# Fewer sevenfold pairs in the first three blocks of the up-projection, and the convolution queued ahead of the split

## The chip, the cores and the metric

The kernel runs on one core of a Trainium2 chip. The metric is the device time of one execution in microseconds; less is better. Three runs of the kernel before took 1755.26, 1757.42 and 1757.81 us, a median of 1757.42 us.

## What is computed

One layer of a hybrid decoder block on 256 tokens of width 2048, all in float32: a norm, one combined input projection, a gated linear recurrence and a dilated attention, two merge gates and an output projection, and then the part that the change touches:

```python
def conv_ffn(u, w_up, conv_w, conv_b, w_down):
    hup = u @ w_up                                   # 2048 x 11264
    hc = causal_depthwise_conv(hup, conv_w) + conv_b # width 3, along the tokens
    a, b = hc[..., :D_FF], hc[..., D_FF:]            # D_FF = 5632
    return (jax.nn.gelu(a) * b) @ w_down             # 5632 x 2048
```

It is added to the residual, and a last norm follows.

## The kernel before, in words

All weights are read from HBM once, in 1 MB **units** of sixteen 128 x 128 blocks, in the order in which they are used (`stream_spec`). A buffer `raw` holds a unit; there are three. Before use each unit is **split**: ScalarE writes a rounded high part (`hi`), VectorE subtracts it from the weights and writes the low part (`lo`). TensorE forms each product as three matmuls of 512 columns, low by high, high by high, high by low (lines 543 to 545 for w_up, 490 to 492 for w_down), so only the third needs the low part of the weights.

The up-projection runs over 11 **blocks**. A block takes 512 columns of each of the two halves of w_up, and its contraction in 8 **pairs** of 128 rows each, a unit per pair. A pair of type P is 8 products (24 matmuls); its unit is split in two pieces `hl`. A pair of type S is the sevenfold form: 7 products (21 matmuls) of sums of the weight blocks. `split_s` (line 292) forms them with four additions of 128 x 512 on VectorE (lines 304 to 309, the first one named `q`) and splits four pieces `sa`, `se`, `sf` (128 x 1024 each) and `sg` (128 x 512). All 11 blocks alternate S and P by `UP_PAIRS = "SPSPSPSP"`; `up_order` sets the order of the pairs in the first two. The activations of every pair are prepared once, in the form of its type, by `operands` (line 512), while the output projection w_out runs. The products gather in seven PSUM banks, and `unfold` (line 549) reads the seven sums after a block into `c11` to `c22`, three of them by a DMA that accumulates (line 567, POOL's queue).

Some blocks are followed by units of w_down, type P, for hidden blocks that are ready: two after blocks 1 and 2, four after each later one, more at the end. Units are numbered through: block 0 of w_up is 168 to 175, block 1 176 to 183, block 6 232 to 239.

The hidden values of a block are finished while later units run, by a generator, `hidden_side` (line 988): it waits `HIDDEN_WAIT = 3` units, and then takes a step per unit: two steps `ua t0`, `ua t1` for the first half and two `ub t0`, `ub t1` for the second (`convolve`, line 970). In a step TensorE transposes four 128 x 128 blocks into PSUM bank 8 (line 978), ScalarE makes two scaled copies (line 981) and VectorE adds the two other taps to each (lines 982 and 983). There is one bank 8, so the next step's transposes must wait for VectorE. After the four steps come a GELU, a product (line 1001) and the split of the result `ff` (line 1005, through 282).

`begin_unit(u)` (line 370) comes ahead of each unit's matmuls: it writes the splits of the units up to `u + LOOKAHEAD` (2), starts the load of unit u + 3, and then lets the generator take its step:

```python
    def begin_unit(u):
        for v in range(u, u + LOOKAHEAD + 1):
            split(v)
        load(u + LOOKAHEAD + 1)
        pump(SIDE_US)
```

A scheduler of the framework sets the final order on each engine, by the program's order and its own estimates; `in_turn` pins instructions of an engine behind a given one of that engine. Split pieces go through a ring of six buffers (`pair_tile`, line 284), so a split can lead TensorE by about two units at most.

Of the kernel before, what the change touches and what calls it, by code (L numbers as in the profile page):

```python
# [15 lines left out]
ALU = mybir.AluOpType  # L16
# [32 lines left out]
START_X = {0: ((2, 4),), 1: ((4, 8),), 2: ((8, 12),), 3: ((12, 16),)}  # L49


def up_order(b):


    return {0: (1, 3, 0, 5, 2, 4, 7, 6), 1: (1, 0, 3, 2, 5, 4, 6, 7)}.get(b, tuple(range(KD // 2)))

# [1 line left out]
def stream_spec():  # L60
    spec, modes = [], {}

    def stat(name, col, k0, nk):
        for k in range(k0, k0 + nk):
            spec.append((name, k * P, col))

    def mov(name, col, k0, nk):
        for k in range(k0, k0 + nk):
            for c in range(4):
                spec.append((name, k * P, col + c * P))  # L70

    def pairs(name, n1, n2, k0, modes_of, order):

        for i in order:
            mode = modes_of[i]
            assert len(spec) % UNIT == 0
            k2, k1 = k0 + 2 * i, k0 + 2 * i + 1
            modes[len(spec) // UNIT] = mode
            blocks = [(k1, n1), (k2, n1), (k2, n2), (k1, n2)] if mode == "S" else [(k1, n1), (k2, n1), (k1, n2), (k2, n2)]
            for k, n in blocks:  # L80
                for c in range(4):
                    spec.append((name, k * P, n + c * P))

    o_q, o_f, o_i, o_g = 0, 2048, 4096, 6144
    o_aq, o_ak, o_av, o_ga, o_gb = 8192, 9728, 11264, 12800, 14848
    for k in range(KD):
        for base in (o_av, o_aq):
            for c in range(AH):
                spec.append(("w_in", k * P, base + c * P))
    for h in range(AH):  # L90
        stat("w_in", o_ak + h * P, 0, KD)
    for j in range(1, AG):
        for base in (o_aq, o_ak):
            for h in range(AH):
                stat("w_in", base + (j * AH + h) * P, 0, KD)
        mov("w_in", o_av + j * 512, 0, KD)
    for g in range(NGRP):
        for base in (o_f, o_q):
            for h in range(HG):
                stat("w_in", base + (g * HG + h) * P, 0, KD)  # L100
        mov("w_in", o_i + g * 512, 0, KD)
        mov("w_in", o_g + g * 512, 0, KD)
    for base in (o_ga, o_gb):
        for j in range(NJ):
            mov("w_in", base + j * 512, 0, KD)
    for j in range(NJ):
        mov("w_proj_b", j * 512, 0, AH)
        mov("w_proj_a", j * 512, 0, KD)
    for j in range(NJ):
        mov("w_out", j * 512, 0, KD)  # L110
    for b in range(NBLK):
        pairs("w_up", b * 512, DFF + b * 512, 0, UP_PAIRS, up_order(b))
        for j, b0, b1 in DOWN.get(b, ()):
            mov("w_down", j * 512, b0 * FB, (b1 - b0) * FB)

    for j in range(NJ):
        mov("w_down", j * 512, (NBLK - 1) * FB, FB)
    assert len(spec) % UNIT == 0
    return spec, modes
# [56 lines left out]
def hybrid_block(ctx, tc, x_p, x_t, weights, g1, gf, params, c_rope, c_mask0, c_mask1, c_level, out):  # L176
# [52 lines left out]

    raws, splits, late = {}, {}, {}  # L230
    ring = [0]
    last = [None, None]

    @contextmanager
# [133 lines left out]
        debt[0] = 0.0  # L368

    def begin_unit(u):  # L370
        for v in range(u, u + LOOKAHEAD + 1):
            split(v)
        load(u + LOOKAHEAD + 1)
        pump(SIDE_US)

    def next_pair():

# [134 lines left out]
    def operands(a, mode, i, name):  # L512

        f = a.rearrange("p k m t -> p (k m) t")
        if mode == "S":
            x = stage(f"{name}x32_{i}").rearrange("p (b t) -> p b t", b=4)
            vec.tensor_tensor(x[:, 0:2], f[:, 3:4].to_broadcast([P, 2, P]), f[:, 1:3], op=ALU.subtract)
            vec.tensor_tensor(x[:, 2], f[:, 2], x[:, 0], op=ALU.subtract)
            vec.tensor_tensor(x[:, 3], f[:, 0], x[:, 2], op=ALU.subtract)
            parts = w4([2, 3, P], f"{name}s{i}", F32R), w4([2, 4, P], f"{name}x{i}", F32R)  # L520
            two_parts(parts[0][:, 0], parts[0][:, 1], f[:, 0:3])
            two_parts(parts[1][:, 0], parts[1][:, 1], x)
            names = ("a12", "a22", "a11"), ("x1", "x3", "x2", "x4")
        else:
            d = stage(f"{name}d32_{i}")[:, :T].rearrange("p (k t) -> p k t", k=2)
            vec.tensor_tensor(d, a[:, :, 0], a[:, :, 1], op=ALU.subtract)
            parts = w4([2, 4, P], f"{name}a{i}", F32R), late["hv"].tile([P, 2, 2, P], F32R, tag=f"{name}d", name=f"{name}d{i}", bufs=sum(m != "S" for m in UP_PAIRS))
            two_parts(parts[0][:, 0], parts[0][:, 1], f)
            two_parts(parts[1][:, 0], parts[1][:, 1], d)
            names = ("a12", "a22", "a11", "a21"), ("d2", "d1")  # L530
        return {n: (t[:, 0, j], t[:, 1, j]) for t, ns in zip(parts, names) for j, n in enumerate(ns)}
# [438 lines left out]
    def convolve(ups, c0, t, name):  # L970


        for i in range(2):
            pt = late_bank(8, f"{name}t{i}").rearrange("p (c t) -> p c t", c=2)
            for c in range(2):
                for m in range(2):
                    n = (2 * i + c) * P
                    pe.transpose(pt[:, c, m * P : (m + 1) * P], ups[m][:, n : n + P], ident)
            for c in range(2):
                d, s, col = t[:, 2 * i + c], pt[:, c], c0 + 2 * i + c  # L980
                act.activation(d, s, AF.Identity, bias=pc("cb", col), scale=pc("cw2", col))
                vec.scalar_tensor_tensor(d[:, 1:], s[:, : T - 1], pc("cw1", col), d[:, 1:], op0=ALU.mult, op1=ALU.add)
                vec.scalar_tensor_tensor(d[:, 2:], s[:, : T - 2], pc("cw0", col), d[:, 2:], op0=ALU.mult, op1=ALU.add)
            yield SIDE_US

    ff = {}
# [1 line left out]
    def hidden_side(b, sums):  # L988

        c11, c21, c12, c22 = unfold(sums, rstd2, neg2, f"up{b}")  # L990
        for _ in range(HIDDEN_WAIT):
            yield SIDE_US
        a, g = (late["pool"].tile([P, FB, T], F32, tag="uc", name=f"u{n}{b}", bufs=2) for n in "ab")
        yield from convolve((c11, c21), b * FB, a, f"ua{b}")
# [14 lines left out]
        return t[:, 0, m * P : (m + 1) * P], t[:, 1, m * P : (m + 1) * P]  # L1009

    for b in range(NBLK):
        sums = sevenfold(hv, UP_PAIRS, up_order(b), f"up{b}")
        drain()
        side.append(hidden_side(b, sums))
        pump(0.0001)
        for j, b0, b1 in DOWN.get(b, ()):
            pst = moving(ff_parts, b0 * FB, (b1 - b0) * FB, f"dn{b}_{j}", [late_bank(i, f"dn{b}_{j}_{i}") for i in ((4, 3) if j % 2 else (1, 5))])
            for m in range(2):
                if b == NBLK - 1:
                    vec.tensor_tensor(ht[j][:, m], ht[j][:, m], pst[m], op=ALU.add)  # L1020
                else:
                    t = stage(f"dns{b}_{j}_{m}")
                    act.activation(t, pst[m], AF.Copy)
                    nc.gpsimd.dma_start(ht[j][:, m], t, accum_op=ALU.add)
# [84 lines left out]
```

## Time and profile before

| | |
|---|---|
| median of three runs | 1757.42 us |
| profiled execution, its own time | 1757.53 us |
| its span | 1755.8 us |
| TensorE busy | 1725.8 us, 98% of the span |
| VectorE busy | 1302.6 us, 74% |
| ScalarE busy | 992.8 us, 57% |
| DMA | 346.13 MB, mean 197 GB/s |
| mean granted clock of TensorE | 0.995 |

The profiled execution took 1757.53 us, 0.11 us more than the median of the runs; its span, from the first to the last instruction, is 1755.8 us, and 1.7 us lie outside it. TensorE's line gives little away, since it is busy nearly throughout: what is left are its waits, and the stretches in which the clock was below full speed. VectorE's 74% is a mean; in the up-projection, from 1008 us to the end, it is far busier than earlier.

### The profile page before, as it was taken

The page shows a single profiled execution, that of the slowest core. Times are in us where ns is not written, and L with a number is a line of the kernel's source. Part 1 is how long each engine was busy: PE and PEld are TensorE (multiplying, and loading weights), DVE is VectorE, ACT ScalarE, POOL GpSimd, SP SyncE. Part 2 cuts the span into 40 slices and gives each one's busy share as a digit, 9 for nine tenths or more (in the row PEclk, how much of TensorE's full clock was granted, in tenths as well). Part 3 has the DMA queues.
Part 4 walks back from the last instruction along what each step waited for, and adds up shares of the span by engine and source line. Part 5 has one row for each costly group of instructions (what it writes and reads, how often), then busy time and mean ns, then how long its engine had stood idle before and what let it go on. Part 6 is the DMA issues. An engine that isn't in the chain of part 4 may idle for free.

```text
span 1755.8 us, 21521 instructions
## 1 busy us (share of the span) xinstructions
PE 1725.8 (98%) x8340; PEld 1440.9 (82%) x8340; DVE 1302.6 (74%) x1628; ACT 992.8 (57%) x1259; POOL 70.2 (4%) x94
## 2 busy tenths in 40 slices
PE   9999999999999999999999999799999999999998
PEld 7888888888888888888888877688878878788886
DVE  7765575877768675445665699899978978889977
ACT  6444465545454555444444577576666666566663
POOL 0000000000000000000000000110010010010000
PEclk9999999999999999999999999899999999999999
DMA  7665634544444444556555546687677586676672
GB/s 276 236 212 197 219 144 148 185 162 177 166 167 171 159 177 168 183 195 243 178 186 191 189 185 204 176 234 239 188 234 242 182 235 234 189 231 224 204 257 96
DMA packets 58310, 346.13 MB, mean 197 GB/s; under 512 B 6704, under 2 KB 6960, under 8 KB 20064
## 3 DMA queue, kind: packets, MB, share of 16 engines
q1 hardware_dynamic: 45504, 318.02, 51.2%
q0 software_dynamic: 11408, 23.34, 6.7%
q10 hardware_dynamic: 1296, 3.41, 0.5%
q8 instruction: 65, 1.06, 0.2%
q14 instruction: 37, 0.30, 0.0%
HBM read 321.41 MB, written 2.10 MB: 184 GB/s over the span
## 4 chain that ended last, share of the span: by engine, by line
PE 84%; DVE 7%; DMA 6%; ACT 2%; issue 1%; DVEq 0%; SPq 0%; ACTq 0%; POOLq 0%
PE up L545 6%; PE up L543 6%; PE up L544 6%; DMA raw<-weights 6%; PE egp L491 3%; PE egp L490 3%; PE egp L492 3%; PE dn L490 3%; PE dn L492 3%; PE dn L491 3%; PE ak L403 3%; DVE hl L337 2%; PE aq L403 2%; PE gp L492 2%; PE wo L490 2%; PE gp L490 2%
## 5 line engine op out<-in xcount | busy, mean ns | idle before, releaser
L337 DVE TENSOR_TENSOR hl<-raw,hl 128x1024 fp32r<-128x1024 f32 (+1 forms) x510 | 618.4, 1218 | 311.8 <-ACT hl L336 310.2
L336 ACT ACTIVATE hl<-raw 128x1024 fp32r<-128x1024 f32 (+1 forms) x510 | 534.8, 1054 | 526.0 <-PE egp L492 79.4
L490 PE MATMUL dn<-hl,ff 128*128 128x512 f32 x320 | 127.5, 398 | 0.0
L491 PE MATMUL dn<-hl,ff 128*128 128x512 f32 x320 | 125.9, 393 | 0.0
L492 PE MATMUL dn<-hl,ff 128*128 128x512 f32 x320 | 125.4, 393 | 0.0
L543 PE MATMUL up<-hl,hva 128*128 128x512 f32 x264 | 103.1, 391 | 1.6 <-ACT up0e L566 1.6
L545 PE MATMUL up<-hl,hva 128*128 128x512 f32 x264 | 103.0, 390 | 0.0
L544 PE MATMUL up<-hl,hva 128*128 128x512 f32 x264 | 102.9, 390 | 0.0
L490 PE MATMUL egp<-hl,xu 128*128 128x512 f32 x256 | 100.5, 393 | 0.0
L492 PE MATMUL egp<-hl,xu 128*128 128x512 f32 x256 | 99.8, 390 | 0.0
L491 PE MATMUL egp<-hl,xu 128*128 128x512 f32 x256 | 99.7, 389 | 0.0
L492 PEld LDWEIGHTS dn<-hl,ff 128*128 128x128 f32 x320 | 60.8, 190 | 13.0
L490 PEld LDWEIGHTS dn<-hl,ff 128*128 128x128 f32 x320 | 61.0, 190 | 12.6 <-DVE up2c L571 0.5
L491 PEld LDWEIGHTS dn<-hl,ff 128*128 128x128 f32 x320 | 60.9, 190 | 12.3
L403 PE MATMUL ak<-xu,hl 128*128 128x512 f32 x192 | 67.1, 394 | 0.0
L282 DVE TENSOR_TENSOR sa<-raw,sa 128x1024 fp32r<-128x1024 f32 x44 | 53.6, 1219 | 15.4 <-ACT sa L281 15.4
L543 PEld LDWEIGHTS up<-hl,hva 128*128 128x128 f32 x264 | 49.6, 188 | 12.1 <-ACT up0e L566 2.0
L281 ACT ACTIVATE sf<-raw 128x1024 fp32r<-128x1024 f32 x44 | 46.3, 1053 | 22.1 <-DVE raw L309 8.9
L545 PEld LDWEIGHTS up<-hl,hva 128*128 128x128 f32 x264 | 49.6, 188 | 10.3
L544 PEld LDWEIGHTS up<-hl,hva 128*128 128x128 f32 x264 | 49.6, 188 | 10.2
L282 DVE TENSOR_TENSOR se<-raw,se 128x1024 fp32r<-128x1024 f32 x44 | 53.7, 1221 | 4.7 <-ACT se L281 4.7
L281 ACT ACTIVATE sa<-raw 128x1024 fp32r<-128x1024 f32 x44 | 46.4, 1055 | 18.4 <-PE up L545 12.2
(559 smaller groups left out, 4218.2 us busy)
## 6 DMA issues: line engine op xcount, KB each, us to landing
raw<-weights SPq DMA_DIRECT2D x298, 1024.0 KB, 4.8
h<-dns POOLq DMA_DIRECT2D x36, 256.0 KB, 7.5
h<-x_t ACTq DMA_DIRECT2D x4, 512.0 KB, 4.9
xt<-x_p SPq DMA_DIRECT2D x3, 512.0 KB, 10.1
xs_q<-aqraw POOLq DMA_DIRECT2D x6, 256.0 KB, 7.2
xs_k<-akraw POOLq DMA_DIRECT2D x6, 256.0 KB, 7.2
raw<-weights SPq DMA_DIRECT2D x2, 512.0 KB, 6.9
gfb<-gf POOLq DMA_DIRECT2D x2, 512.0 KB, 10.6
```

The lines of the kernel that those rows point to most:

```text
L281: act.activation(hi, src, AF.Copy)
L282: vec.tensor_tensor(lo, src, hi.bitcast(F32), op=ALU.subtract)
L336: last[0] = act.activation(hi[:, q * w : (q + 1) * w], raw, AF.Copy)
L337: last[1] = vec.tensor_tensor(lo[:, q * w : (q + 1) * w], raw, hi[:, q * w : (q + 1) * w].bitcast(F32), op=ALU.subtract)
L403: pe.matmul(ps, hi, pair, start=(k == 0), stop=False, skip_group_check=True)
L490: pe.matmul(pst[m], xl, hi, start=(k == k0), stop=False)
L491: pe.matmul(pst[m], xh, hi, start=False, stop=False)
L492: pe.matmul(pst[m], xh, lo, start=False, stop=(k == k0 + nk - 1))
L543: pe.matmul(sums[b], xl, wh, start=b in fresh, stop=False)
L544: pe.matmul(sums[b], xh, wh, start=False, stop=False)
L545: pe.matmul(sums[b], xh, wl, start=False, stop=left[b] == 0)
```

## The change

In block 0 only pairs 4 and 6 stay sevenfold, in blocks 1 and 2 pairs 2, 4 and 6; the other blocks keep four. Pairs 0 and 2, which are now of one type in some blocks and of the other in others, have both sets of operands prepared (`BOTH`). The order of the pairs in the first two blocks changes. In the last part of the kernel `begin_unit` lets the generator step first, and pins the splits written after it behind the last VectorE instruction of that step. The first hidden block waits two units in place of three.

```diff
+def up_modes(b):
+    return {0: "PPPPSPSP", 1: "PPSPSPSP", 2: "PPSPSPSP"}.get(b, UP_PAIRS)
+
+BOTH = (0, 2)
 
 def up_order(b):
-    return {0: (1, 3, 0, 5, 2, 4, 7, 6), 1: (1, 0, 3, 2, 5, 4, 6, 7)}.get(b, tuple(range(KD // 2)))
+    return {0: (1, 3, 0, 2, 5, 4, 7, 6), 1: (1, 0, 2, 3, 4, 5, 6, 7)}.get(b, tuple(range(KD // 2)))
...
-        pairs("w_up", b * 512, DFF + b * 512, 0, UP_PAIRS, up_order(b))
+        pairs("w_up", b * 512, DFF + b * 512, 0, up_modes(b), up_order(b))
...
+    conv = [None]
...
     def begin_unit(u):
-        for v in range(u, u + LOOKAHEAD + 1):
-            split(v)
+        conv[0] = None
+        if "pool" in late:
+            pump(SIDE_US)
+
+        with in_turn(*(conv[0] or ())):
+            for v in range(u, u + LOOKAHEAD + 1):
+                split(v)
         load(u + LOOKAHEAD + 1)
-        pump(SIDE_US)
+        if "pool" not in late:
+            pump(SIDE_US)
...
             two_parts(parts[0][:, 0], parts[0][:, 1], f[:, 0:3])
             two_parts(parts[1][:, 0], parts[1][:, 1], x)
             names = ("a12", "a22", "a11"), ("x1", "x3", "x2", "x4")
+            if i in BOTH:
+                d = stage(f"{name}d32_{i}")[:, : 3 * P].rearrange("p (k t) -> p k t", k=3)
+                vec.tensor_tensor(d[:, :2], a[:, :, 0], a[:, :, 1], op=ALU.subtract)
+                vec.tensor_copy(d[:, 2], f[:, 3])
+                parts += (w4([2, 3, P], f"{name}b{i}", F32R),)
+                two_parts(parts[2][:, 0], parts[2][:, 1], d)
+                names += (("d2", "d1", "a21"),)
...
-                vec.scalar_tensor_tensor(d[:, 2:], s[:, : T - 2], pc("cw0", col), d[:, 2:], op0=ALU.mult, op1=ALU.add)
+                conv[0] = (
+                    vec.scalar_tensor_tensor(d[:, 2:], s[:, : T - 2], pc("cw0", col), d[:, 2:], op0=ALU.mult, op1=ALU.add),
+                )
...
-        for _ in range(HIDDEN_WAIT):
+        for _ in range(HIDDEN_WAIT - (b == 0)):
...
-        sums = sevenfold(hv, UP_PAIRS, up_order(b), f"up{b}")
+        sums = sevenfold(hv, up_modes(b), up_order(b), f"up{b}")
```

How the instructions move, at three places. Names carry a unit's number (`sa232` is a piece of unit 232, `hl237_0` of unit 237) and, after the last underscore, a buffer's.

VectorE, around the convolution step `ua5t0`, four units after block 5's pairs end. `q232` to `sf232` is the split of unit 232, an S pair of block 6, two units later. Before:

```order
L304 TENSOR_TENSOR q232_10411<-raw232_10377 128x512
L306 TENSOR_TENSOR raw232_10377<-raw232_10377 128x512
L337 TENSOR_TENSOR hl231_1_10374<-raw231_10345,hl231_1_10374 128x1024
L282 TENSOR_TENSOR sg232_10425<-q232_10411,sg232_10425 128x512
L282 TENSOR_TENSOR sa232_10413<-raw232_10377,sa232_10413 128x1024
L307 TENSOR_TENSOR raw232_10377<-q232_10411,raw232_10377 128x512
L309 TENSOR_TENSOR raw232_10377<-raw232_10377 128x512
L282 TENSOR_TENSOR se232_10418<-raw232_10377,se232_10418 128x1024
L982 SCALAR_TENSOR_TENSOR ua5_10430<-ua5t0_10432,par_85,ua5_10430 128x255
L304 TENSOR_TENSOR q234_10523<-raw234_10473 128x512
L983 SCALAR_TENSOR_TENSOR ua5_10430<-ua5t0_10432,par_85,ua5_10430 128x254
L306 TENSOR_TENSOR raw234_10473<-raw234_10473 128x512
```

With the change:

```order
L1004 SCALAR_TENSOR_TENSOR ua5_10391<-ua5t0_10393,par_85,ua5_10391 128x255
L1006 SCALAR_TENSOR_TENSOR ua5_10391<-ua5t0_10393,par_85,ua5_10391 128x254
L1004 SCALAR_TENSOR_TENSOR ua5_10391<-ua5t0_10393,par_85,ua5_10391 128x255
L1006 SCALAR_TENSOR_TENSOR ua5_10391<-ua5t0_10393,par_85,ua5_10391 128x254
L313 TENSOR_TENSOR q232_10404<-raw232_10357 128x512
L291 TENSOR_TENSOR sa232_10406<-raw232_10357,sa232_10406 128x1024
L315 TENSOR_TENSOR raw232_10357<-raw232_10357 128x512
L316 TENSOR_TENSOR raw232_10357<-q232_10404,raw232_10357 128x512
L291 TENSOR_TENSOR sg232_10418<-q232_10404,sg232_10418 128x512
L291 TENSOR_TENSOR se232_10411<-raw232_10357,se232_10411 128x1024
L318 TENSOR_TENSOR raw232_10357<-raw232_10357 128x512
L1004 SCALAR_TENSOR_TENSOR ua5_10391<-ua5t1_10447,par_85,ua5_10391 128x255
```

The whole step `ua5t0` and the first half of `ua5t1` now stand ahead of the last piece of unit 232; before, most of the split of unit 232 stood ahead of the step, and its last piece in the middle of it.

TensorE, at the end of unit 236 (S) and the begin of unit 237 (P) in block 6. Before:

```order
L543 MATMUL up6_6_10521<-sf236_10629,hvx4_7501 128x512
L544 MATMUL up6_6_10521<-sf236_10629,hvx4_7501 128x512
L545 MATMUL up6_6_10521<-sf236_10629,hvx4_7501 128x512
L543 MATMUL up6_4_10519<-sf236_10629,hvs4_7500 128x512
L544 MATMUL up6_4_10519<-sf236_10629,hvs4_7500 128x512
L545 MATMUL up6_4_10519<-sf236_10629,hvs4_7500 128x512
L543 MATMUL up6_5_10520<-sg236_10632,hvx4_7501 128x512
L544 MATMUL up6_5_10520<-sg236_10632,hvx4_7501 128x512
L545 MATMUL up6_5_10520<-sg236_10632,hvx4_7501 128x512
L543 MATMUL up6_2_10517<-hl237_0_10665,hva5_7516 128x512
```

With the change (lines 565, 566, 567 are the former 543, 544, 545):

```order
L565 MATMUL up6_5_10500<-sg236_10619,hvx4_7513 128x512
L566 MATMUL up6_5_10500<-sg236_10619,hvx4_7513 128x512
L565 MATMUL up6_6_10501<-sf236_10616,hvx4_7513 128x512
L566 MATMUL up6_6_10501<-sf236_10616,hvx4_7513 128x512
L565 MATMUL up6_4_10499<-sf236_10616,hvs4_7512 128x512
L566 MATMUL up6_4_10499<-sf236_10616,hvs4_7512 128x512
L567 MATMUL up6_5_10500<-sg236_10619,hvx4_7513 128x512
L565 MATMUL up6_2_10497<-hl237_0_10645,hva5_7528 128x512
L567 MATMUL up6_6_10501<-sf236_10616,hvx4_7513 128x512
L567 MATMUL up6_4_10499<-sf236_10616,hvs4_7512 128x512
```

The matmuls that need only a high part (565, 566) now go ahead of those that need a low one (567) over several products.

TensorE, at the first transposes of the first hidden block, in block 1. Before:

```order
L543 MATMUL up1_5_8044<-sg177_7991,hvx0_7161 128x512
L544 MATMUL up1_5_8044<-sg177_7991,hvx0_7161 128x512
L545 MATMUL up1_5_8044<-sg177_7991,hvx0_7161 128x512
L978 MATMUL ua0t0_8129<-ident_87,up0c21_8022 128x128
L978 MATMUL ua0t0_8129<-ident_87,up0c11_8021 128x128
L978 MATMUL ua0t0_8129<-ident_87,up0c21_8022 128x128
```

With the change:

```order
L566 MATMUL up1_3_8027<-hl176_1_7944,hvd1_7183 128x512
L567 MATMUL up1_3_8027<-hl176_1_7944,hvd1_7183 128x512
L1000 MATMUL ua0t0_8077<-ident_87,up0c11_8006 128x128
L565 MATMUL up1_2_8026<-hl177_0_7973,hvs0_7160 128x512
L566 MATMUL up1_2_8026<-hl177_0_7973,hvs0_7160 128x512
L565 MATMUL up1_5_8029<-hl176_1_7944,hva1_7182 128x512
L566 MATMUL up1_5_8029<-hl176_1_7944,hva1_7182 128x512
L567 MATMUL up1_5_8029<-hl176_1_7944,hva1_7182 128x512
L565 MATMUL up1_5_8029<-hl176_1_7944,hva1_7182 128x512
L566 MATMUL up1_5_8029<-hl176_1_7944,hva1_7182 128x512
L567 MATMUL up1_5_8029<-hl176_1_7944,hva1_7182 128x512
L567 MATMUL up1_2_8026<-hl177_0_7973,hvs0_7160 128x512
```

The first transposes now stand within unit 176, the first of block 1; before, the last three of these four stood behind unit 177.

## Rows read from the trace of the kernel before

**Rows 1.** Waits of TensorE, 1000 to 1756 us: waiter, releaser, total, times, longest.

```profile
PE ua1t L978 <- DVE ff L282: 3.9, 1, 3.9
PE up L543 <- ACT sa L281: 3.8, 1, 3.8
PE ua7t L978 <- DVE ua L983: 3.1, 1, 3.1
PE up L543 <- ACT up0e L566: 1.6, 1, 1.6
PE ub1t L978 <- DVE ua L983: 1.5, 1, 1.5
PE ua6t L978 <- DVE ua L983: 1.3, 1, 1.3
```

**Rows 2.** Windows: length, then busy us of PE, PEld, DVE, ACT, POOL; clock.

```profile
1050.00:1166.00 116.00, 103.59 (x452) 82.64 (x451) 103.23 (x137) 77.97 (x102) 9.68 (x12) 0.96 0.66 206
1293.60:1626.00 332.40, 325.74 (x1461) 266.84 (x1460) 285.57 (x356) 214.00 (x271) 30.73 (x35) 0.99 0.70 217
1359.90:1424.50 64.60, 64.60 (x293) 53.18 (x292) 56.14 (x71) 42.84 (x55) 6.14 (x7) 1.00 0.70 221
1100.00:1110.00 10.00, 4.13 (x12) 2.88 (x13) 8.02 (x13) 4.38 (x7) 1.72 (x2) 0.59 0.71 170
1500.00:1510.00 10.00, 8.28 (x34) 6.80 (x35) 6.30 (x10) 5.28 (x8) 1.77 (x2) 0.83 0.41 138
```

**Rows 3.** Timeline of TensorE, 1098 to 1140 us: start, duration.

```profile
1109.09 0.63 PE L492 MATMUL dn<-hl,ff 128*128 128x512 f32 x1
1109.52 0.63 PE L490 MATMUL dn<-hl,ff 128*128 128x512 f32 x1
```

**Rows 4.** Timeline of TensorE, 1394 to 1399 us (unit 236, then 237).

```profile
1396.16 0.39 PE L544 MATMUL up<-sf,hvx 128*128 128x512 f32 x1
1396.39 0.39 PE L545 MATMUL up<-sf,hvx 128*128 128x512 f32 x1
...
1398.43 0.39 PE L545 MATMUL up<-hl,hva 128*128 128x512 f32 x1
```

**Rows 5.** Timeline of VectorE, 1390 to 1398 us.

```profile
1389.70 0.68 DVE L304 TENSOR_TENSOR q<-raw 128x512 f32<-128x512 f32 x1
1390.30 0.47 DVE L983 SCALAR_TENSOR_TENSOR ub<-ub5t,par,ub 128x254 f32<-128x254 f32 x1
1390.69 1.22 DVE L282 TENSOR_TENSOR sf<-raw,sf 128x1024 fp32r<-128x1024 f32 x1
1391.83 1.22 DVE L1001 TENSOR_TENSOR ub<-ua,ub 128x1024 f32<-128x1024 f32 x1
1392.96 1.22 DVE L337 TENSOR_TENSOR hl<-raw,hl 128x1024 fp32r<-128x1024 f32 x1
```

**Rows 6.** Timeline of VectorE, 1355 to 1367 us (unit 232, convolution ua5).

```profile
1364.84 1.22 DVE L282 TENSOR_TENSOR sf<-raw,sf 128x1024 fp32r<-128x1024 f32 x1
1365.97 0.48 DVE L982 SCALAR_TENSOR_TENSOR ua<-ua5t,par,ua 128x255 f32<-128x255 f32 x1
1366.49 0.48 DVE L983 SCALAR_TENSOR_TENSOR ua<-ua5t,par,ua 128x254 f32<-128x254 f32 x1
```

**Rows 7.** Timeline of ScalarE, 1355 to 1370 us.

```profile
1359.40 1.33 ACT L1023 ACTIVATE dns<-dn 128x512 f32<-128x512 f32 x2 [0.93 <-PE dn L492]
...
1361.58 0.56 ACT L981 ACTIVATE ua<-ua5t,par 128x256 f32<-128x256 f32 x1
```

**Rows 8.** Timeline of VectorE, 1484 to 1512 us.

```profile
1494.50 0.48 DVE L982 SCALAR_TENSOR_TENSOR ua<-ua7t,par,ua 128x255 f32<-128x255 f32 x1
1497.84 0.69 DVE L304 TENSOR_TENSOR q<-raw 128x512 f32<-128x512 f32 x1 [2.86 <-DMA raw<-weights]
1498.45 0.48 DVE L983 SCALAR_TENSOR_TENSOR ua<-ua7t,par,ua 128x254 f32<-128x254 f32 x1
```

**Rows 9.** DMA issues, 1040 to 1130 us: count, size, median us to landing.

```profile
up0c<-up0e POOLq DMA_DIRECT2D x3, 256.0 KB, 4.0
up1c<-up1e POOLq DMA_DIRECT2D x3, 256.0 KB, 5.3
```

## The prediction

> **What bounds the kernel now.** I read the busy shares first: TensorE 98%, VectorE 74%, ScalarE 57%. TensorE is the bound in the mean, so the change can gain only from TensorE's waits, and it pays for each matmul that it adds. The second view is the list of those waits in the up-projection [rows 1]. Three kinds stand there: transposes of a convolution step (`ua1t`, `ua7t`, `ub1t`, `ua6t`) that wait for VectorE, sevenfold products that wait for a split (`sa`), and one that waits for the reading of a PSUM sum (`up0e`). The third view gives the size by stretch [rows 2]: from 1050 to 1166 us TensorE is busy 103.59 of 116 us, so 12.4 us idle; from 1293.6 to 1626 us it is busy 325.74 of 332.4 us, so 6.7 us idle over five blocks. The window from 1359.9 to 1424.5 us, in which block 5's convolution runs beside block 6, has none: 64.60 of 64.60. After the long waits the granted clock is below full speed, 0.59 from 1100 to 1110 us and 0.83 from 1500 to 1510 us. A matmul step there takes 1109.52 - 1109.09 = 0.43 us [rows 3], against 1396.39 - 1396.16 = 0.23 us (0.2267 as a mean over many) in a warm stretch [rows 4]; the two steps are those of the 1.2 and the 2.4 GHz level. Nine such steps follow the wait at 1106 us, five that near 1500 us.
>
> Why do transposes wait for VectorE? [Rows 8] show the worst case. L982 of a step ran at 1494.50, then stood `q`, the first addition of a later unit's split, which waited 2.86 us for its weights, and only behind it, at 1498.45, came L983 of the same step. Bank 8 is free only after the step's last L983, so TensorE stood for 3.1 us [rows 1]. The order of VectorE's queue made the stall, not the work in it.
>
> **The sum, part by part.** It starts from the profiled 1757.53 us, which is 0.1 us above the median.
>
> *Types.* Four pairs become P (two in block 0, one each in blocks 1 and 2): 4 x 3 = 12 more matmuls x 0.2267 = **+2.7 us** on TensorE, on the path. VectorE drops four sevenfold splits for plain ones. A sevenfold one is four additions of 0.6 us, three pieces of 1.13 and one of some 0.6, 6.4 us; a plain one is two pieces of 1.13 (1.22 as shown with their pipelining) [rows 5], 2.3 us: 4.1 us less each, in the stretch where the idle time is greatest. I take this and the convolution's new place to remove the waits of 1050 to 1166 us (types: `sa`, `up0e`, `ff`): **-12.4 us**. The lower end is nothing, if the waits only move.
>
> *Convolution first.* A step now stands ahead of the split of unit u+2, so a `q` that waits for weights can't hold it. This removes the 6.7 us of transposes' waits in 1293.6 to 1626 us: **-6.7 us**. With the two long waits go the cold steps behind them: (9 + 5) x (0.43 - 0.23) = **-2.8 us**.
>
> That gives 1757.5 + 2.7 - 12.4 - 6.7 - 2.8 = 1738.3 us, if nothing new waits. Three things are new.
>
> *The first hidden block waits two units in place of three.* Its transposes now come within unit 176. The sums `c11` and `c21` are finished by the accumulating DMAs, 4.0 to 5.3 us from issue to landing [rows 9], after some 2.8 us of evictions of 128 x 512 on VectorE and ScalarE. Between the pairs' end and the transposes stand 18 matmuls ahead of the first, 29 ahead of the later ones: 4.1 and 6.6 us by 0.2267 each. Between none and 4 us of a wait; I take **+1.5 us**, in the lower half because half of the four transposes stand behind the 29.
>
> *The split waits for the transposes.* VectorE now can't begin the split of unit u+2 before TensorE and ScalarE have finished with the step. Take `ua5t0`. In before, ScalarE's read of `dns` ends at 1359.40 + 1.33 = 1360.7, and the first scaled copy could end 0.56 later [rows 7], at 1361.3. Four taps cost 0.5 + 0.4 + 0.5 + 0.4 = 1.8 us, by the two taps and the step between their starts [rows 5, 6], to 1363.1; then comes unit 232's split, 6.4 us, and in it two taps of `ua5t1`, 0.9. So `sf232` ends at 1370.4, where it ended at 1364.84 + 1.22 = 1366.06: 4.3 us later. By then four taps have been done, 1.8 us that before came after, while `q` and the second addition of unit 234, 1.2 us, which had been done, have not: 3.7 us of real lag. Dependent pairs of instructions, which can't overlap, add some 0.5: **4.2 us**.
>
> The cover: `sf236` was there at 1390.69 + 1.22 = 1391.91 and its first user, the third matmul, came at 1396.39, 4.5 us later; `hl237_0` at 1392.96 + 1.22 = 1394.18 and used at 1398.43, 4.25 us later [rows 4, 5]. The lag just fits. TensorE's new order takes matmuls that need only high parts ahead of those that need a low one, four steps at that place, 4 x 0.227 = 0.9 us more cover. Against it, each of the three later convolution steps can delay VectorE by up to one copy of ScalarE, 0.56 us [rows 7], so up to 1.7 us. One block's window thus costs w: from 0 to 1.7 us. I take w = 0.6, a third, since a VectorE that is busy 56.14 of 64.6 us [rows 2] recovers 8 us over a block and the cover is refilled between steps. Ten windows, the convolutions of blocks 1 to 10: **+6.0 us**. Ends: 0 and 17 us.
>
> *Edits at no cost.* Two pairs' operands in both forms are 1 us of VectorE and 0.5 of ScalarE each, in the output projection, where no wait of TensorE is listed and VectorE idles; without that cover, 2 us. The order of transfers on SP's queue and of the accumulating DMAs on POOL's stays as it was. The load of unit u + 3 is still issued behind the splits.
>
> Sum: 1738.3 + 1.5 + 6.0 = **1745.8 us**, so 1746.
>
> **Rivals.**
>
> *No difference: the reordered matmuls give no cover.* Then w is nearly its full 1.7, say 1.65: 1738.3 + 1.5 + 16.5 = 1756.3 us. For it: the lag of 4.2 us is within 0.3 us of a cover of 4.25 to 4.5, and the sums behind it carry errors of half a microsecond. Against: in block 5's window VectorE has 8 us idle.
>
> *Slower: late splits make late loads.* A raw buffer is free when the last reader of its split is done. If that is 4 us later in each window, the load of unit u + 3 starts 4 us later; in before one `q` already waited 2.86 us for its weights [rows 8]. If each window brings a third of this, 1.0 us, on top of w = 1.65, w is 2.65 and the time 1738.3 + 1.5 + 26.5 = 1766.3 us. It decides from w = (1757.5 - 1738.3 - 1.5) / 10 = 1.77 on. For it: with three raw buffers a lost lead isn't made up within the window, and whatever stands behind a convolution that waits, waits too. The Trainium skill, "TensorE: Matmul & The Clock Gate", section "Architectural detail", says that VectorE's and ScalarE's queues are strictly first in, first out; TensorE pulls ahead only weight loads. By that rule a split pinned behind a tap that waits for TensorE can't slip past it, which speaks against this change; the trace agrees, as L983 at 1498.45 stood behind the 2.86 us of `q`. Against the rival: DMA is busy 0.70 of the time in these windows [rows 2], not full.
>
> *It does less than it says.* The next step's transposes need bank 8, which is one, whatever the queue's order. If the waits of blocks 3 and later (6.7 us and 1.0 us of their cold steps) remain, as the tap itself and not its place is late, only the first blocks gain: 1745.8 + 7.7 = 1753.5 us. For it: `ua6t` and `ub1t` wait only 1.3 and 1.5 us [rows 1], too short to blame on a long queue.
>
> **How the numbers follow.** About 0.2%, 3.5 us, is what a measurement of this kernel can tell from no change: faster is below 1753.9, slower above 1760.9. The forecast has a chance of 0.52, no difference 0.17, the slower rival 0.17, the partial one 0.14. The last lies at the edge of "faster": two thirds of it, 0.10, go there and 0.04 to "same". So faster 0.62, same 0.21, slower 0.17. The range runs from 1738, no new wait at all, to 1763, w = 2.3, most of the way to the slower rival; beyond lies half of that rival's 0.17, below a few per cent.
>
> **What would show it.** Right: no wait of `ua1t` on `ff`, of `up` on `sa` or `up0e`, or of `ua7t` on L983 is left over 1 us; the list of waits gains L545's new lines (567) waiting on `sf`, `se` or `hl`, some 6 us in all; the granted clock from 1100 to 1110 us is above 0.9; the window of block 5's convolution shows about 64 us of work in a length of 65. Wrong: waits of 567 on low parts of more than 15 us in all, or waits of the split's first addition on weights in many blocks, show that the new order costs what it gives; transposes still waiting on the last tap in blocks 5 to 8 show that the partial rival was right. The unknown that weighs most is w, ten times over.

## The result: slower by 0.56%, and the profile after

| | before | changed |
|---|---|---|
| median of six runs each, same chip | 1755.51 us | 1764.92 us (1760.95 to 1767.27) |
| ratio | | 1.0056, 95% interval 1.0039 to 1.0073 |
| profiled execution, its own time | 1757.53 us | 1760.95 us |
| TensorE busy | 1725.8 us | 1731.7 us |
| VectorE busy | 1302.6 us | 1287.5 us |

The forecast was 1746 us; the slower rival stood at 1766.3. The two profiled executions lie only 3.4 us apart, since the one of before was slow for its kernel and the one of after was the fastest of its six; what that hides is taken up below, at the "-6.7" of the sum.

TensorE's waits in the changed kernel, 1000 to 1760 us (waiter, releaser, total, times, longest), answer to [rows 1]:

```profile
PE ua1t L1000 <- DMA up1c<-up1e: 5.3, 1, 5.3
PE ua3t L1000 <- DMA up3c<-up3e: 5.1, 1, 5.1
PE ua0t L1000 <- DMA up0c<-up0e: 2.1, 1, 2.1
PE up L567 <- DVE sf L291: 1.2, 3, 0.7
PE up L565 <- ACT sf L290: 0.9, 2, 0.7
PE ub9t L1000 <- DVE ua L1006: 0.9, 1, 0.9
```

What was to go is gone: no wait of `ua7t` on a tap, of `up` on `sa` or on `up0e`, of `ua1t` on `ff`. In their place stand three waits of transposes for the accumulating DMA of `c11` and `c21`, of blocks 1, 3 and 0; the one of block 3 had no counterpart before. That is one of the signs of being right that the prediction named; another failed, as the clock from 1100 to 1110 us stayed at 0.78, under the 0.9 named. Its signs of being wrong did not come: matmuls of line 567 wait 1.2 us on low parts, where 15 were named, and no transpose of blocks 5 to 8 waits over 0.8 us for a tap.

The windows (length, busy us of PE, PEld, DVE, ACT, POOL, clock, DMA share, GB/s) answer to [rows 2]:

```profile
1050.00:1166.00 116.00, 107.57 (x472) 86.11 (x471) 94.15 (x123) 72.70 (x96) 9.74 (x12) 0.97 0.59 186
1100.00:1110.00 10.00, 4.73 (x17) 3.58 (x16) 6.40 (x7) 5.36 (x8) 2.64 (x3) 0.78 1.03 320
1205.00:1235.00 30.00, 24.95 (x104) 20.05 (x103) 19.84 (x22) 17.40 (x23) 3.51 (x4) 0.89 0.72 240
1293.60:1626.00 332.40, 330.00 (x1475) 266.91 (x1474) 285.95 (x358) 214.24 (x272) 30.89 (x35) 1.00 0.68 221
```

From 1050 to 1166 us TensorE still idles 8.4 us (12.4 before). Between 1205 and 1235 us it loses 5.05 us at one place, and the clock is 0.89 there. From 1293.6 to 1626 us it idles 2.4 us (6.7 before): this part of the change worked.

TensorE's timeline at the new stall (start, duration):

```profile
1218.57 0.39 PE L506 MATMUL dn<-hl,ff 128*128 128x512 f32 x1
1224.01 0.45 PE L1000 MATMUL ua3t<-ident,up3c 128*128 128x128 f32 x1 [5.05 <-DMA up3c<-up3e]
1224.11 0.78 PE L507 MATMUL dn<-hl,ff 128*128 128x512 f32 x1
1224.68 0.63 PE L505 MATMUL dn<-hl,ff 128*128 128x512 f32 x1
1225.11 0.63 PE L506 MATMUL dn<-hl,ff 128*128 128x512 f32 x1
```

One single transpose stands in the middle of the first w_down unit behind block 3, and everything behind it waits until 1224.01. Ten slow matmul steps follow, most of 0.43 us (1225.11 - 1224.68), some 2 us more in all than at the 2.4 GHz level. Before, the same transposes ran at 1229.01, all four together, two units behind the block, and waited for nothing:

```profile
1229.01 0.60 PE L978 MATMUL ua3t<-ident,up3c 128*128 128x128 f32 x4
```

The order of TensorE's instructions in the changed kernel shows the same place (it was readable before the result was):

```
L505 MATMUL dn3_0_1_9285<-hl205_0_9230,ff2_0_9123 128x512
L506 MATMUL dn3_0_1_9285<-hl205_0_9230,ff2_0_9123 128x512
L1000 MATMUL ua3t0_9361<-ident_87,up3c11_9266 128x128
L507 MATMUL dn3_0_1_9285<-hl205_0_9230,ff2_0_9123 128x512
```

Counted from its block's last product, the first transpose is the 11th instruction on TensorE in block 1, the 13th in block 3, the 19th in block 0, and the 49th in every other block (so 18 matmuls stand between in block 0, as the prediction has it); in the kernel before the 49th from block 2 on, the 3rd in block 1 and the 16th in block 0.

POOL's timeline says when `up3c` could be there: the DMA of `c11`, which the lone transpose reads, is issued at 1213.63, those of `c21` and `c12` only at 1221.21, when VectorE has read `c21` for `c22` (L592).

```profile
1213.63 0.87 POOL L589 DMA_DIRECT2D up3c<-up3e  x1 [37.67 <-ACT up3e L588]
1221.21 1.77 POOL L589 DMA_DIRECT2D up3c<-up3e  x2 [6.71 <-DVE up3c L592]
```

The three take a median of 9.9 us to land here (7.8 in the kernel before, where nothing waited for them), those of block 1 8.4 (5.3 before, [rows 9]). With the 5.3 us of [rows 9] the DMA of 1213.63 would have landed at 1218.9, just when the transpose's turn came (1218.57 + 0.39).

The other cost is the late splits. VectorE's timeline of the changed kernel, unit 232 and `ua5t0`, answers to [rows 6]:

```profile
1367.05 0.48 DVE L1004 SCALAR_TENSOR_TENSOR ua<-ua5t,par,ua 128x255 f32<-128x255 f32 x1 [2.18 <-ACT ua L1003]
...
1368.69 0.48 DVE L1004 SCALAR_TENSOR_TENSOR ua<-ua5t,par,ua 128x255 f32<-128x255 f32 x1 [0.63 <-ACT ua L1003]
1369.20 0.48 DVE L1006 SCALAR_TENSOR_TENSOR ua<-ua5t,par,ua 128x254 f32<-128x254 f32 x1
1369.60 0.68 DVE L313 TENSOR_TENSOR q<-raw 128x512 f32<-128x512 f32 x1
...
1376.23 1.23 DVE L291 TENSOR_TENSOR sf<-raw,sf 128x1024 fp32r<-128x1024 f32 x1 [0.28 <-ACT sf L290]
```

VectorE stands 2.18 us for the first scaled copy and 0.63 for the second; only behind the last tap begins the split. Over the whole up-projection, 1000 us to the end, VectorE waits 47.5 us for the scaled copies of `ua` and `ub`, where it waited 3.0; its `q` waits less for weights than before. The changed kernel, then the one before:

```profile
DVE ua L1004 <- ACT ua L1003: 37.6, 33, 4.8
DVE ub L1004 <- ACT ub L1003: 9.9, 13, 1.6
DVE q L313 <- DMA raw<-weights: 3.8, 5, 1.4
```

```profile
DVE q L304 <- DMA raw<-weights: 16.1, 11, 3.2
DVE ua L982 <- ACT ua L981: 1.6, 4, 0.7
DVE ub L982 <- ACT ub L981: 1.4, 1, 1.4
```

In unit 232 `sf` is there at 1377.46. TensorE uses it first at 1380.98, 3.5 us later; before it was there at 1366.06 and used at 1375.07, 9.0 us later:

```profile
1380.98 0.39 PE L565 MATMUL up<-sf,hvx 128*128 128x512 f32 x1
```

```profile
1375.07 0.39 PE L543 MATMUL up<-sf,hvx 128*128 128x512 f32 x1
```

Where 5.5 us of lead are lost, the later units of the block are hit. Little of that is in TensorE's list of waits; the list for its weight loads, 1240 to 1760 us, shows more (the kernel with the splits free, below, has no such row there):

```profile
PEld up L567 <- DVE sf L291: 3.0, 6, 1.1
PEld up L567 <- DVE hl L346: 1.4, 4, 0.5
PEld up L565 <- ACT sf L290: 1.4, 4, 0.7
```

The rest are steps of 0.3 to 0.6 us between matmuls of 512 columns, in place of 0.23: 45 of them over units 208 to 279 (blocks 4 to 9 and their w_down), 4.4 us in excess, against 24 (2.1 us) with the splits free. Of these 45, 18 stand beside a weight load that waits 0.25 to 1.1 us for a split piece.

### The profile page after: what moved, and what is told of

The parts are those of the page before. It is cut to its first block, busy times and chain, and to the rows that moved or that the text cites. A ratio compares the mean times of both kernels' runs of the same rounds, so it can differ in the third digit from the quotient of the medians.

```text
span 1759.2 us, 21482 instructions
## 1 busy us (share of the span) xinstructions
PE 1731.7 (98%) x8352; PEld 1442.1 (82%) x8352; DVE 1287.5 (73%) x1610; ACT 984.6 (56%) x1253; POOL 70.3 (4%) x94
## 4 chain that ended last, share of the span: by engine, by line
PE 87%; DMA 4%; DVE 4%; issue 3%; ACT 1%; DVEq 0%; SPq 0%; ACTq 0%; POOLq 0%
PE up L567 7%; PE up L565 7%; PE up L566 7%; PE egp L507 3%; PE egp L506 3%; PE egp L505 3%; PE dn L507 3%; PE dn L505 3%; PE dn L506 3%; PE ak L418 3%; DMA raw<-weights 2%; PE aq L418 2%; PE gp L507 2%; PE gp L505 2%; PE wo L507 2%
## 5 line engine op out<-in xcount | busy, mean ns | idle before, releaser
L345 ACT ACTIVATE hl<-raw 128x1024 fp32r<-128x1024 f32 (+1 forms) x518 | 540.3, 1053 | 499.2 <-PE egp L507 79.4
L290 ACT ACTIVATE sf<-raw 128x1024 fp32r<-128x1024 f32 x40 | 42.3, 1057 | 41.1 <-DVE raw L318 41.0
L290 ACT ACTIVATE se<-raw 128x1024 fp32r<-128x1024 f32 x40 | 42.3, 1058 | 33.3 <-DVE raw L315 32.9
L507 PEld LDWEIGHTS egp<-hl,xu 128*128 128x128 f32 x256 | 48.1, 188 | 9.9
L506 PEld LDWEIGHTS egp<-hl,xu 128*128 128x128 f32 x256 | 48.1, 188 | 9.8
```

Of the source, the lines that this page charges most:

```text
L290: act.activation(hi, src, AF.Copy)
L345: last[0] = act.activation(hi[:, q * w : (q + 1) * w], raw, AF.Copy)
L506: pe.matmul(pst[m], xh, hi, start=False, stop=False)
L507: pe.matmul(pst[m], xh, lo, start=False, stop=(k == k0 + nk - 1))
```

## The experiments

All are built from the changed kernel or from the one before, by the edit named. The ratios are to the kernel before, measured beside them on the same chip (1754.51 us for the first four; 1753.28 us for `types_pin`, `pin_free`, `before_pin` and `after_again`; 1754.42 us for the last four). The first four ran on another chip than the rest, so across that line ratios are compared, and not medians.

**The first transposes pinned** (`pin`).

```diff
-                pe.matmul(sums[b], xh, wl, start=False, stop=left[b] == 0)
+                mm[0] = pe.matmul(sums[b], xh, wl, start=False, stop=left[b] == 0)
...
+            with in_turn(*(() if i or name[1] == "b" else mm)):
-            for c in range(2):
-                for m in range(2):
+                for c in range(2):
+                    for m in range(2):
```

(`mm[0]` is set in `moving_step` as well; the four transposes stand inside the `with`.)

> The changed kernel, with the first transposes of each hidden block (step t0 of the first half) pinned behind the last matmul of the unit ahead of them; on TensorE's queue the first transpose of blocks 1 and 3 then stands 47 and 49 matmuls behind its block's last product in place of 11 and 13. Theory A (the loss is TensorE standing at early transposes until the accumulating DMA of c11 lands): the waits of 5.3 and 5.1 us go, and with them the ten cold steps of 0.2 us excess behind each, 4.0 us; the 2.1 us of block 0 stay. From a median of 1764.9: 1750 to 1751 us, faster than the kernel before (1755.5). Theory B (the loss is the splits that now come late behind the convolution): the order of the splits is as in the changed kernel, so 1762 to 1766 us.

Measured: 1751.18 us, ratio 0.9981 (0.9970 to 0.9993). The waits are as theory A had them; block 0's stays:

```profile
PE ua0t L1002 <- DMA up0c<-up0e: 1.5, 1, 1.5
PE ua4t L1002 <- DMA up4c<-up4e: 0.6, 1, 0.6
PE ua3t L1002 <- DMA up3c<-up3e: 0.2, 1, 0.2
```

By the two ratios (1.0056 and 0.9981), some 13 us of the time hung on the place of two single transposes: on every other engine the order of the instructions is that of the changed kernel, and on TensorE these two stand 36 places later, and a few products of blocks 2 and 3 some places off.

**The convolution's new place alone** (`conv_only`): old types, old orders, `HIDDEN_WAIT` 3 for all blocks.

> The kernel before with the convolution ahead of the split alone (old types, old order of pairs, three units of waiting for every block). Its first transposes stand at 49 matmuls in every block but the first. Theory A: the waits of ua1t (3.9 and 0.7 us, with 1.8 us of cold steps) and the transposes' waits of the later blocks (6.7 us with 1.0 of cold steps) go, the waits for sa (3.8) and up0e (1.6) stay, late splits cost about 0.3 us a block: 1743 to 1748 us. Theory B: late splits cost as much as in the changed kernel, so 1758 us or more.

Measured: 1757.53 us, ratio 1.0021 (1.0009 to 1.0034). A miss for theory A, and within 0.5 us of theory B: from block 1 on there are no early transposes here, and it is still no faster. What it waits for are the low parts:

```profile
PE up L567 <- DVE hl L346: 3.9, 2, 2.9
PE up L567 <- DVE sf L291: 2.1, 2, 1.6
PE up L565 <- ACT up0e L588: 1.6, 1, 1.6
PE ub8t L1000 <- DVE ua L1006: 1.5, 1, 1.5
```

So the pin on the splits has a price of its own, and it is dearest in block 1, where four sevenfold splits stand behind the taps: 5.9 us over units 182 and 183 (times of the last products in the two profiles), 1.6 in the changed kernel.

**Types and orders alone** (`types_only`): `begin_unit` as before, `HIDDEN_WAIT` 3.

> The kernel before with the new types and the new order of pairs alone (splits ahead of the convolution as before, three units of waiting). The first transposes of block 1 stand 7 matmuls behind its last product (3 before), those of the other blocks at 49. Theory A: 2.7 us more matmuls, the waits for sa (3.8) and up0e (1.6) gone, the wait of ua1t and of the later blocks' transposes as before: 1751 to 1755 us. Theory B: the types have no part in the loss either: the same.

Measured: 1749.48 us, ratio 0.9972 (0.9959 to 0.9986), better than expected by 1.5 us. `sa` and `up0e` are gone from the list; the transposes' waits stay:

```profile
PE ua7t L994 <- DVE ua L1000: 3.5, 1, 3.5
PE ua1t L994 <- DMA up1c<-up1e: 2.3, 1, 2.3
PE ua1t L994 <- DVE ub L1019: 2.3, 1, 2.3
```

**The suspected cost for every block** (`wait2all`).

```diff
-        for _ in range(HIDDEN_WAIT - (b == 0)):
+        for _ in range(HIDDEN_WAIT - 1):
```

> The changed kernel with two units of waiting for every hidden block, not only the first: the first transpose stands 11 to 13 matmuls behind its block's last product in blocks 1 to 9. Theory A: eight more blocks (2, 4 to 9, and 10 in part) wait some 5 us each for the accumulating DMA, with 2 us of cold steps behind: 1764.9 + 8 x 7 = about 1820 us. Theory B (late splits): the convolution comes a unit earlier, the order against the splits is the same: within 5 us of the changed kernel.

Measured: 1805.68 us (one run). Eleven blocks wait for their accumulating DMA, 1.4 to 5.4 us each, 40 us in all:

```profile
PE ua1t L1000 <- DMA up1c<-up1e: 5.4, 1, 5.4
PE ua7t L1000 <- DMA up7c<-up7e: 5.4, 1, 5.4
...
PE ua6t L1000 <- DMA up6c<-up6e: 1.7, 1, 1.7
PE ua0t L1000 <- DMA up0c<-up0e: 1.4, 1, 1.4
```

The mechanism is theory A's; the size is 41 us, not 55, as a block waits 3.6 us on average and not 5. The expectation also had the places wrong: in blocks 6 to 10 the first transpose is the 25th instruction behind the block, not the 11th to 13th, and still waits.

**Types with the pinned transposes** (`types_pin`): `types_only` and the edit of `pin`.

> New types and order of pairs and the pinned first transposes, with the splits written ahead of the convolution as in the kernel before. Against the run types alone (1749.5) the first transposes of block 1 stand at 55 matmuls and not at 7: its waits of 2.3 and 2.3 us and five cold steps (1.0 us) go, 1744 us. Against the run with the pin (1751.2) it lacks only the convolution's new place. Theory C (the new place costs 0.9 us a block in late splits, nine us in all, and gives back the transposes' waits on the taps, 5 to 8 us): 1744 to 1750 us. Rival (the new place is a net gain of the 8 us that were forecast, and only the early transposes hid it): 1757 us or more.

Measured: 1750.53 us, ratio 0.9985 (0.9974 to 0.9997). In theory C's range, but not the 1744 of the sum: the pin brought nothing here. The 4.6 us of `ua1t` came back as

```profile
PE dn L500 <- DVE ff L292: 4.7, 1, 4.7
```

The hidden block 0 was late as such; the transposes were only the first to stand in the queue. Against the rival: without the convolution's new place the ratio is that of `pin` (0.9985 and 0.9981). The two differ in one thing more than the expectation says: block 0 waits three units here and two in `pin`. That does not decide it, as `conv_only`, with three units and the new place, gains 12.6 us over units 184 and 185 in the profiles, like `pin` (12.8), where `types_pin` gains 4.0. What the new place gains there it loses elsewhere, 4.0 us of it over units 168 to 183 (`pin` 2.2 behind the kernel before, `types_pin` 1.8 ahead). So the new place, in the form of the change, is worth nothing in the sum.

**The splits free** (`pin_free`): `pin`, and

```diff
-        with in_turn(*(conv[0] or ())):
+        with in_turn():
```

> The run with the pinned transposes (1751.2), but the splits are no longer pinned behind the last tap; the convolution is only written first, so that the scheduler is free to set the two against each other. On VectorE most of the split of unit 232 stands ahead of ua5t0 again. Theory C: the late splits' cost (some 9 us over the blocks) mostly goes, the taps still come a little earlier than before: 1744 to 1748 us. Rival (the cost lies with the early steps, not with the splits behind them): 1750 to 1753 us.

Measured: 1743.39 us, ratio 0.9945 (0.9931 to 0.9959), 6.3 us below `pin` by the ratios (7.8 by the medians). The convolution is still written first; only its last tap no longer holds the splits.

**The kernel before with the pinned transposes** (`before_pin`).

> The kernel before with the pinned first transposes alone (old types, old order). In block 1 they move from 3 to 52 matmuls behind the last product; elsewhere they stood at 46 to 49 already. The wait of ua1t (3.9 and 0.7 us) and its cold steps (1.8 us) should go: 1754.5 - 6.4 = 1748 us. Rival (the block 1 stall is VectorE's load, which moves to the next wait): 1753 to 1756 us.

Measured: 1749.92 us, ratio 0.9980 (0.9967 to 0.9992). Between the two: `ua1t` is gone, but `dn` waits 4.3 us for `ff`, and in the profiles only 2.0 us are gained over units 184 and 185.

```profile
PE dn L500 <- DVE ff L292: 4.3, 1, 4.3
```

**The changed kernel once more** (`after_again`).

> The changed kernel once more, for a second profile: its profiled execution (1760.95) was the fastest of its six, with a median of 1764.9. If the early transposes' waits vary with the landing of the accumulating DMA, a slower execution shows longer waits of ua1t and ua3t, or one in another block; if the spread comes from elsewhere, these waits are 5.3 and 5.1 again.

Measured: 1762.50 us, and the waits of `ua1t`, `ua3t` and `ua0t` are 4.9, 4.8 and 2.3 us. They belong to the kernel, as far as two profiles show; the spread of its runs stays unexplained.

**One line undone** (`free`): the changed kernel with the edit of `pin_free`, without that of `pin`.

> The changed kernel with one line undone: the splits are still written after the convolution step, but no longer pinned behind its last tap. The scheduler then puts the first transposes of blocks 1 and 3 at 49 matmuls behind the block's last product by itself (11 and 13 in the changed kernel; block 0 stays at 19 and 31), and on VectorE most of a split ahead of the taps. Theory D (both losses, the early transposes and the late splits, come from this pin): as the run with the transposes pinned and the splits free, 1742 to 1746 us. Rival (the transposes' pin did something more): 1749 us or more.

Measured: 1745.18 us, ratio 0.9942 (0.9926 to 0.9958), theory D. All four transposes of block 3 run together again, at 1220.88, without a wait:

```profile
1220.88 0.60 PE L1000 MATMUL ua3t<-ident,up3c 128*128 128x128 f32 x4
```

By the two ratios (1.0056 and 0.9942), some 20 us of the changed kernel's time hang on this one `in_turn`. With the splits free the pin on the transposes changes nothing: `free` and `pin_free` have the same instructions in the same order on every engine. Their two times, 1745.18 and 1743.39 us, are thus two measurements of one program, and show what a difference of 2 us is worth.

**Three units of waiting for block 0** (`pin_free3`): `pin_free` with `HIDDEN_WAIT` for all.

> The run with the transposes pinned and the splits free (1743.4), with three units of waiting for block 0 as for the others: its first transposes stand at 49 matmuls, not 19 and 31. If only the landing of the accumulating DMA counts: the 1.4 us of ua0t go, 1742 us. Rival (a unit's delay makes the split of ff of block 0 late for the w_down products behind block 1, where two runs with three units waited 4.3 and 4.7 us with 2 us of cold steps): 1748 to 1750 us.

Measured: 1742.07 us (four runs, 1739.26 to 1749.00), ratio 0.9921 (0.9904 to 0.9939), the fastest of the study by median, though `conv_free`, `pin_free` and `free` lie at most 3.1 us above and the intervals overlap. The profile is that of the slowest of the four, 1749.00 us. `ua0t` is out of the list, and `dn` waits 0.9 us for `ff` where the rival had 4.3 to 4.7: with the convolution written first, the block is nearly in time.

**`c11` and `c21` finished by VectorE** (`acc_dve`): the changed kernel, early transposes and pinned splits included.

```diff
-        add_scaled(c11, p[2], r0, 2)
+        vec.scalar_tensor_tensor(c11, p[2], r0, c11, op0=ALU.mult, op1=ALU.add)
...
-        add_scaled(c21, p[4], r1, 4)
+        vec.scalar_tensor_tensor(c21, p[4], r1, c21, op0=ALU.mult, op1=ALU.add)
```

> The changed kernel, with the last terms of c11 and c21 added by VectorE from PSUM (two operations of 0.75 us a block) in place of a copy by ScalarE and an accumulating DMA; c12 keeps its DMA. The first transposes still stand at 13 (block 0), 25 (block 1) and 13 (block 3) matmuls. If it is the DMA's landing that the early transposes wait for: the waits of ua0t, ua1t and ua3t (2.1, 5.3, 5.1 us) fall under 2 us each and their cold steps go, while the late splits stay: 1748 to 1753 us. Rival (early transposes wait for VectorE's queue as well, or the added work makes the splits later still): 1757 us or more.

Measured: 1750.89 us, ratio 0.9978 (0.9966 to 0.9991). The waits of `ua0t`, `ua1t` and `ua3t` are gone altogether, with the first transposes still the 13th instruction behind the block in blocks 0 and 3, and the 25th in block 1. It was the landing of the DMA that they had waited for. What stays are the late splits:

```profile
PE up L565 <- ACT sf L290: 2.1, 3, 0.8
PE up L567 <- DVE sf L291: 1.8, 2, 1.5
PE ub4t L1000 <- DVE ua L1006: 1.6, 1, 1.6
```

**The convolution written first, the transposes pinned, and no more** (`conv_free`): `pin_free` with old types, old orders and `HIDDEN_WAIT` 3.

> The run with the transposes pinned and the splits free (1743.4), with the old types, the old order of pairs and three units for block 0: the convolution written first, and nothing else of the change. It tells what the types are worth once the pin is gone: 2.7 us of matmuls less, but the waits for sa (3.8) and up0e (1.6) are back, and the product with ff may be late (4.3 us with cold steps): 1746 to 1751 us. Rival (the types bring nothing): 1741 to 1743 us.

Measured: 1742.71 us, ratio 0.9927 (0.9914 to 0.9941): the rival. The wait for `sa` did not come back (`up0e` did, 1.6 us), and the types, worth 5 us alone, are worth nothing that four runs of each can show beside `pin_free3` (1742.07 us, 0.9904 to 0.9939). Both kernels take most of their gain over units 184 and 185, 11.3 and 11.1 us in the profiles: it is the same stall, and it can be removed but once. The pinned transposes belong to this kernel: without them its first transpose of block 1 would stand right behind the block's last product, and that was not run.

## Why the prediction was wrong, point by point

What each stretch of the program gained or lost in the profiled executions, in us against the kernel before, by the start of the last product of a unit:

| units | changed | `pin` | `pin_free` |
|---|---|---|---|
| up to 167 | -0.2 | +1.2 | +0.9 |
| 168 to 183 | +2.8 | +2.2 | -0.3 |
| 184, 185 | -5.3 | -12.8 | -12.6 |
| 186 to 203 | +0.7 | +1.9 | +2.3 |
| 204, 205 | +7.4 | +0.5 | 0.0 |
| 206 to 299 | -2.0 | -1.2 | -5.7 |
| sum | +3.4 | -8.2 | -15.4 |

**The step that failed: the convolution's place was priced on VectorE alone.** The prediction let the convolution move against the splits, and asked for TensorE's transposes against their accumulating DMA only in block 0, where `HIDDEN_WAIT` said so. But the step that is written earlier can also be queued earlier on TensorE: the scheduler put one transpose of block 3 36 matmuls further up (49th to 13th), and that of block 1 at the 11th place. Why it chose these two, no run shows. The term is missing from the sum: 5.1 us and some 2 us of cold steps in block 3 (+7.4 in the table). The landing time that the prediction took from [rows 9], 4.0 to 5.3 us, holds for the first two blocks alone; in block 3 it was 7.8 us in the kernel before already. In block 1 the missing term ate what "-12.4" and the cold steps had booked: through unit 203 the changed kernel is 2.0 us ahead with its 2.7 us of added matmuls paid, a gain of 4.7 us where 12.4 + 1.8 = 14.2 were booked. The prediction had named the lower end of this term, "nothing, if the waits only move"; they moved from `ff` (3.9) and `sa` (3.8) to `up1c` (5.3). `pin` and `acc_dve` each take this away by another means and agree, ratios 0.9981 and 0.9978; `pin` gets back 7.5 us over units 184 and 185 and 6.9 over 204 and 205. By stretch, the profile lies 15.1 us above the forecast's sum: 6.8 through unit 203 (8.8 forecast as a gain there, with block 0 and two windows of w), 7.4 in units 204 and 205, and 0.9 behind them.

**"+1.5" for block 0:** 2.1, 2.3, 1.5 us in three profiles. Right, and by its own mechanism.

**"-6.7" and the cold steps of the later blocks:** units 218 and 219, 242 and 243, 254 and 255, 266 and 267 gained 1.2, 2.0, 4.7 and 0.8 us, 8.7 in all for 7.7 forecast. Right in the profile. But half of it, the stall near 1500 us, comes and goes. From unit 244 on `before_pin` has the instructions of the kernel before in the same order on every engine, and its profile is without the stall (4.5 us gained over units 254 and 255); `types_only`, written in the old order too, has it (`ua7t`, 3.5 us), and `types_pin` has not. Where it stands, a `q` between the taps waits 2.86 us ([rows 8]) and 3.63 us for its weights; in the other two at most 0.55. How many executions of the kernel before have it, no run tells. The profiled execution of before lies 2.0 us above its median and that of the changed kernel 4.0 below, so the medians part by 9.4 us where the profiles part by 3.4. Of this difference of 6.0 the stall can explain no more than the first 2.0. The 4.0 stay open: the second profile of the changed kernel, at 1762.50 us, shows the same three waits.

**w = 0.6, ten times:** 206 to 299 lost 8.7 - 2.0 = 6.7 us, 1.0 on average over seven blocks (4 to 10), and units 182 and 183 of block 1 another 1.6, which the prediction had not counted. The lag at unit 232 was 5.5 us where the working had 4.2: the four taps took 2.6 us and not 1.8, as the second copy was waited for, and the split with its two taps 7.9 and not 7.3. By this reckoning w lies between the forecast and the "no difference" rival. Taken directly, `pin` against `pin_free` prices the pin on the splits at 6.3 us by the ratios (their intervals leave some 3 us either way), 0.6 for each of ten windows, which is the forecast's w; the profiles give 7.2, of which 2.5 stand in units 168 to 183.

**The slower rival** came near in time (1766.3) by another mechanism. It wanted late loads, and the loads came no later: no wait of TensorE for weights is in the list, and those of `q` fell from 16.1 to 3.8 us. In it, the sentence that what is queued behind a waiting convolution waits too held for TensorE, which the prediction had not looked at, as much as for VectorE: behind one transpose 36 matmuls stood that needed nothing from it. The Trainium skill ("TensorE: Matmul & The Clock Gate", section "Step-by-step: what each phase is for") says that matmuls stay in program order and only weight loads are pulled ahead. The trace agrees: in the 5.05 us before 1224.01 no matmul ran.

**+2.7 for twelve matmuls:** over units 168 to 171 and 172 to 175, a changed pair in each, 0.5 us were lost for 0.7 forecast. **The operands in both forms** cost nothing that shows: up to unit 167 the difference is -0.2 us, and in the other profiles it lies between -0.2 and +1.7 us, with and without these operands.

## What to carry to other kernels

Where a step is written earlier, look at every engine that it issues on, and count the instructions between the last product that its inputs hang on and its first instruction there. Here a lone transpose, 13 matmuls (3 us) behind its block on an input whose DMA took about 10 us to land, cost 7.4 us, more than the 6.7 us of stalls that the move was to remove in the later blocks. Set a priority by the order in which things are written, and keep a pin for what must not pass: written first, with its first transposes pinned in place and no split held behind it, the convolution gained 11.7 us (`conv_free`), and with the splits pinned behind it lost 3 (`conv_only`). A stall that stands in one profile may be missing in the next, with the same order of instructions; take two before it is booked.

## What the runs showed of the hardware

An accumulating DMA of 256 KB took a median of 4.0 us to land in block 0 of the kernel before, 5.3 in block 1, and 7.7 to 11.4 in blocks 3 to 9. In block 1 of the changed kernel it was 8.4, while the DMA share from 1100 to 1110 us had risen from 0.71 [rows 2] to 1.03. That the one comes from the other was not tested.

Weight loads that wait a few tenths of a microsecond for a split piece don't all show as waits of TensorE, but as steps of 0.3 to 0.6 us between matmuls: over units 208 to 279 the changed kernel has 21 more of these than `pin_free`, 2.3 us, beside a list of waits of 3.3 us from 1240 us on.
